# Second norm beside the output projection, early FFN loads, and a last down pass by column halves

## The chip, the cores and the metric

The kernel is one program that runs on all 8 cores of one Trainium2 chip at the same time. Each core computes half of one of the four samples; the cores do not exchange data. The metric is the device time of the slowest core, in microseconds (us). Such a program has two states. In the fast one all cores run alike. In the slow one the cores of a die, or of both, show a lower granted clock in the records and the time is longer.

I write PE for TensorE (matmul), ACT for ScalarE, DVE for VectorE, SP for SyncE (which here only issues DMAs) and POOL for GpSimd (which here issues the weight DMAs).

## The reference, cut to what matters

Two layers of a transformer block over 4 samples of 4096 latent tokens and 256 context tokens, width 2048, 12 query heads and 4 key/value heads of 128, FFN width 5632, everything modulated by a conditioning vector.

```python
xn = modulate(rms_norm(h, norm1_g), shift1, scale1)
y  = mixer(xn)                       # layer 0: dense attention + short conv; layer 1: windowed attention + pooling
h  = h + gate1 * (y @ w_out)         # output projection
hn = modulate(rms_norm(h, norm2_g), shift2, scale2)      # the "second norm"
h  = h + gate2 * ((silu(hn @ w_gate) * (hn @ w_up)) @ w_down)
...
return rms_norm(h, final_norm_g)     # after both layers
```

## The kernel before

Everything is kept transposed: 16 chunks of 128 channels on the partitions, tokens in the free dimension. Query blocks have 512 tokens (the last one of layer 0 has 384). One program-order list per engine is built in Python. A "main" generator (attention, FFN, projections) is woven with a "side" queue of generators, at a rate of side steps per main step.

```python
def weave(self, main, rate):
    credit = 0.0
    for _ in main:
        credit += rate
        while credit >= 1.0:
            credit -= 1.0
            if not self.step(): ...
```

The side generator of a block holds the output projection, then the norm of the same block. `Xb` is the residual stream of the block (16 chunks, one buffer), `hnst` two staging buffers of 4 chunks.

```python
def wout_gen(l, b, nblk, F, extra=None):
    for t in range(4):                      # 4 weight tiles w_out
        for c in range(4):                  # 4 output chunks each, 16 matmuls per chunk in 4 steps
            ...                             # DVE: Xb[dch] = psum * gate + Xb[dch]
    for _ in sq_gen(...): yield             # 16 squares (ACT and DVE in turn), 16 ones-matmuls to sum them
    rstd(...)
    for c in range(KD + 1):                 # apply1 on DVE, apply2 on ACT, store hn by 4 chunks
        ...
        if extra is not None and c % 2 == 0: next(extra, None)    # modulation of layer 1
    if b + 1 < nblk: load_Xb(l, b + 1)
```

The FFN of a token block loads all of its input `hn` at its start, runs gate/up and down for each half of the hidden width, and keeps the residual stream in HBM: in the down pass it loads, updates and stores tile by tile. The final norm of the last token block is done after everything else:

```python
side.weave(ffn_gen(side, 1, 1), 0.6)
side.drain()
for _ in final_gen(1):     # load 4 chunks, scale, store, one buffer
    pass
```

Weights come through a ring of three tiles (`NRING = 3`) on the POOL queue; all other transfers are issued by SP, in program order. A store can be held back by some steps: `sc.late(...)`, 24 by default, or until somebody wants to write its source buffer.

## Time and profile before

Before the prediction three runs stood at 7791, 7796 and 7899 us (median 7796.28).

The page of the slowest core, core 5: busy time of each engine in all, then two rows of the view in 40 slices, tenths of PE's busy share and tenths of full clock.

```profile
span 7794.5 us, 101076 instructions; the slowest of 8 cores (7745.4 to 7794.5 us)
...
PE 6943.4 (89%) x35368; PEld 3385.7 (43%) x35368; DVE 2287.2 (29%) x4515; ACT 2295.9 (29%) x3510; POOL 217.0 (3%) x262
...
PE   3889989999976999998999988968789999899992
...
PEclk9989999999998999999999999988889999999996
```

PE is the limit, and it stands still for 851 us of the span. The holes are at the start, in slice 12 (first FFN start), around slices 25 to 30 (layer 1's attention) and at the end. The clock sags where the holes are.

What PE waited for over the whole run, same core (columns: us in total, number of waits, longest):

```profile
PE pair L513 <- ACT arena L1009: 165.4, 181, 6.2
PE pair L513 <- DMA arena<-hn: 87.8, 3, 32.0
...
PE pair L513 <- DMA arena<-w_mod: 61.9, 9, 12.7
PE pair L513 <- DMA arena<-ud: 55.5, 4, 29.4
```

L1009 is the softmax exponential. `hn` is the FFN's input: three long waits, one at each FFN start that was not overlapped. `ud` is the pooling input of layer 1.

Stretches of the same core: from, to and length; busy us (and instructions) of PE, PEld, DVE, ACT and POOL; then granted clock, DMA share and GB/s.

```profile
core 5: us, PE busy (x) PEld busy (x) DVE busy (x) ACT busy (x) POOL busy (x), PEclk, DMA share, GB/s
1268.00:1447.00 179.00, 174.45 (x799) 77.10 (x799) 87.86 (x199) 127.43 (x135) 2.62 (x3) 1.00 0.38 93
1447.00:1562.00 115.00, 100.83 (x493) 41.03 (x493) 70.32 (x161) 102.61 (x124) 4.37 (x5) 0.97 0.80 170
...
5412.00:5553.00 141.00, 108.02 (x515) 49.80 (x515) 70.88 (x156) 68.73 (x142) 3.50 (x4) 0.85 0.68 160
...
7645.00:7794.00 149.00, 0.74 (x2) 0.13 (x2) 31.05 (x64) 4.98 (x6) 0.00 (x0) 0.51 0.36 116
```

The first two rows are one attention block of layer 0. Beside the output projection PE is full; then, beside the norm, ACT is the busiest (103 of 115 us), and over the block all PE waits that are listed are for the softmax exponential on ACT. The third is one block of layer 1, with no engine full. The last is the tail: PE is done, and the chain of waits goes load, scale, store, around and around:

```profile
7776.12 3.56 DMA arena<-hT
7782.11 2.95 DMA outT<-arena
7785.13 3.73 DMA arena<-hT
```

### The profile page before, as it was taken

What the parts mean: (1) busy time and instruction counts of PE and PEld (TensorE: products, weight loads), DVE (VectorE), ACT (ScalarE), POOL (GpSimd) and SP (SyncE); (2) the same over time, 40 slices, a digit from 0 to 9 for tenths busy, and PEclk for the clock granted to TensorE, in tenths of its full rate; (3) what the DMA queues carried; (4) which work ended last, traced back from release to release, by engine and by line L of the source; (5) the groups of instructions that cost most, each with busy time, mean ns of one, the idle gap of its engine ahead of it and who ended that gap; (6) DMA issues with size and microseconds to landing.
All of it is one profiled execution on the core that took longest, in us unless ns stands there. A gap on an engine that the chain in (4) does not pass through costs nothing.

```text
span 7794.5 us, 101076 instructions; the slowest of 8 cores (7745.4 to 7794.5 us)
## 1 busy us (share of the span) xinstructions
PE 6943.4 (89%) x35368; PEld 3385.7 (43%) x35368; DVE 2287.2 (29%) x4515; ACT 2295.9 (29%) x3510; POOL 217.0 (3%) x262
## 2 busy tenths in 40 slices
PE   3889989999976999998999988968789999899992
PEld 1334433343333555554555554433334444344441
DVE  1656455555531111111121113544521101111111
ACT  1655167878841100001110004544521000100000
POOL 0000000000000000000000000000000000000000
PEclk9989999999998999999999999988889999999996
DMA  9546873646676345345565365556764645648463
GB/s 176 142 108 118 144 158 88 140 116 137 138 160 137 71 103 130 65 99 138 99 160 114 64 171 119 116 116 149 154 145 89 156 86 111 136 85 190 93 156 105
DMA packets 486943, 971.21 MB, mean 125 GB/s; under 512 B 46256, under 2 KB 169904, under 8 KB 479024
## 3 DMA queue, kind: packets, MB, share of 16 engines
q0 software_dynamic: 233632, 495.76, 38.3%
q1 hardware_dynamic: 252816, 468.98, 18.8%
q8 instruction: 294, 4.82, 0.2%
q14 instruction: 201, 1.65, 0.1%
HBM read 1277.57 MB, written 182.85 MB: 187 GB/s over the span
## 4 chain that ended last, share of the span: by engine, by line
PE 81%; DMA 8%; ACT 4%; DVE 3%; issue 2%; SPq 2%; DVEq 0%; ACTq 0%; POOL 0%; POOLq 0%
PE pair L513 81%; ACT arena L1009 2%; SPq L199 2%; DMA arena<-w_mod 2%; DMA arena<-hT 2%; DMA arena<-w_in 1%; DMA arena<-hn 1%; DVE arena L587 1%; ACT arena L594 1%; DMA outT<-arena 1%; DMA arena<-w_gu 0%; DMA arena<-ud 0%; DVE arena L1475 0%; DMA arena<-kT 0%; DVE arena L1160 0%
## 5 line engine op out<-in xcount | busy, mean ns | idle before, releaser
L513 PE MATMUL pair<-arena 128*128 128x512 bf16 (+6 forms) x35368 | 6943.4, 361 | 703.7 <-ACT arena L1009 165.4
L513 PEld LDWEIGHTS pair<-arena 128*128 128x128 bf16 (+1 forms) x35368 | 3385.7, 100 | 4260.7 <-issue 1158.2
L1009 ACT ACTIVATE arena<-pair 128x1024 bf16<-128x1024 f32 (+3 forms) x1212 | 1009.6, 865 | 362.3 <-PE pair L513 308.3
L1369 ACT ACTIVATE arena<-pair 128x512 f32<-128x512 f32 (+3 forms) x440 | 239.6, 545 | 2847.0 <-PE pair L513 2847.0
L1372 DVE TENSOR_TENSOR arena<-pair,arena 128x512 bf16<-128x512 f32 (+3 forms) x440 | 274.8, 625 | 2470.5 <-PE pair L513 2461.1
L1018 DVE TENSOR_TENSOR arena<-arena 128x512 bf16<-128x512 bf16 (+2 forms) x1024 | 419.1, 410 | 523.6 <-ACT arena L1009 513.0
L1414 DVE SCALAR_TENSOR_TENSOR arena<-pair,arena 128x512 f32<-128x512 f32 (+3 forms) x352 | 225.7, 642 | 1096.7 <-PE pair L513 1062.9
L594 ACT ACTIVATE arena<-arena 128x512 bf16<-128x512 f32 (+6 forms) x448 | 281.6, 629 | 355.4 <-DVE arena L587 329.8
L587 DVE SCALAR_TENSOR_TENSOR arena<-arena 128x512 f32<-128x512 f32 (+6 forms) x448 | 279.9, 634 | 144.1 <-DMA arena<-hT 54.8
L1425 ACT ACTIVATE arena<-arena 128x1024 bf16<-128x1024 f32 (+2 forms) x64 | 72.8, 1137 | 666.5 <-DVE arena L1414 666.5
L1030 DVE TENSOR_TENSOR arena<-arena 128x512 bf16<-128x512 bf16 (+1 forms) x480 | 198.3, 413 | 63.9 <-DVE arena L1018 21.3
L695 DVE TENSOR_TENSOR arena<-pair,arena 128x512 f32<-128x512 f32 (+2 forms) x180 | 112.4, 625 | 209.7 <-PE pair L513 209.3
L1160 DVE SCALAR_TENSOR_TENSOR arena<-pair,arena 128x512 f32<-128x512 f32 (+2 forms) x160 | 109.5, 684 | 200.6 <-PE pair L513 197.4
L668 ACT ACTIVATE arena<-pair 128x512 bf16<-128x512 f32 (+2 forms) x180 | 97.4, 541 | 193.4 <-PE pair L513 193.4
L199 POOL DMA_DIRECT2D arena<-w_gu x88 | 77.0, 875 | 2413.1 <-PE pair L513 2331.3
L682 DVE SCALAR_TENSOR_TENSOR arena<-pair,arena 128x512 f32<-128x512 f32 (+2 forms) x180 | 122.8, 682 | 34.8 <-ACT arena L677 34.1
L697 DVE TENSOR_TENSOR arena<-arena 128x512 bf16<-128x512 f32 (+2 forms) x180 | 112.9, 627 | 52.8 <-DVE arena L695 31.4
L693 DVE TENSOR_TENSOR arena<-arena 128x512 f32<-128x512 f32 (+2 forms) x180 | 111.6, 620 | 53.0 <-ACT arena L687 52.6
L568 DVE TENSOR_TENSOR arena<-arena 128x512 bf16<-128x512 f32 (+2 forms) x144 | 92.9, 664 | 83.3 <-PE pair L513 56.5
L674 ACT ACTIVATE arena<-pair,arena 128x512 f32<-128x512 f32 (+2 forms) x180 | 113.5, 631 | 0.2 <-PE pair L513 0.2
L565 ACT ACTIVATE arena<-arena 128x512 bf16<-128x512 f32 (+2 forms) x144 | 84.3, 604 | 90.6 <-PE pair L513 62.3
L677 ACT ACTIVATE arena<-arena 128x512 f32<-128x512 f32 (+2 forms) x180 | 104.2, 579 | 16.8 <-ACT arena L674 0.4
(44 smaller groups left out, 852.8 us busy)
## 6 DMA issues: line engine op xcount, KB each, us to landing
arena<-w_gu POOLq DMA_DIRECT2D x88, 2048.0 KB, 15.2
arena<-w_mod POOLq DMA_DIRECT2D x48, 2048.0 KB, 19.7
arena<-w_down POOLq DMA_DIRECT2D x64, 1408.0 KB, 13.9
arena<-w_out POOLq DMA_DIRECT2D x36, 2048.0 KB, 19.8
arena<-hT SPq DMA_DIRECT2D x96, 512.0 KB, 6.3
arena<-w_in POOLq DMA_DIRECT2D x17, 2048.0 KB, 20.7
hT<-arena SPq DMA_DIRECT2D x32, 1024.0 KB, 9.6
hT<-arena SPq DMA_DIRECT2D x64, 512.0 KB, 5.7
```

The costliest lines, as they stand in the source:

```text
L199: e.dma_start(out=it[1], in_=it[2]).then_inc(it[3], 16)
L513: return e.matmul(out, lhsT=lhsT, rhs=rhs, start=start, stop=stop)
L587: sc.op("dve", lambda e, lo=lo, hi=hi, j=j: e.scalar_tensor_tensor(out=ta[:, lo:hi], in0=src[:, lo:hi], scalar=mcol(l, j, ps_, c), in1=rs[ ...
L594: sc.op("act", lambda e, lo=lo, hi=hi, j=j: e.activation(out=dst[:, lo:hi], in_=ta[:, lo:hi], func=AF.Identity, bias=mcol(l, j, pb_, c), s ...
L674: sc.op("act", lambda e: e.activation(out=tr[:, 0:n], in_=banks[SBK][:, 0:n], func=AF.Ln, bias=dcol(DC_CH), scale=1.0), reads=[s_bank[SBK] ...
L682: sc.op("dve", lambda e: e.scalar_tensor_tensor(out=tk[:, 0:n], in0=banks[pb][:, 0:n], scalar=dcol(gcol), in1=tr[:, 0:n], op0=ALU.mult, op ...
L1009: sc.op("act", lambda e: e.activation(out=dst, in_=src, func=AF.Exp, scale=float(ATT_SCALE)), reads=[s_bank[sb(gi, k)] for k in range(nb)] ...
L1018: sc.op("dve", lambda e, a=a % 4, w0=w0, w1=w1, m=m: e.tensor_tensor(out=ps1[a][:, 0:m], in0=P(w0[0], w0[1], m), in1=P(w1[0], w1[1], m), o ...
L1030: sc.op("dve", lambda e, b2=b2, a=arg[0] % 4, c=arg[1] % 4, m=m: e.tensor_tensor(out=ps2[b2][:, 0:m], in0=ps1[a][:, 0:m], in1=ps1[c][:, 0: ...
L1369: sc.op("act", lambda e, i=i, r=r, n=n: e.activation(out=sil[r][:, 0:n], in_=banks[2 * i][:, 0:n], func=AF.Silu), reads=[s_bank[2 * i]], w ...
L1372: sc.op("dve", lambda e, i=i, r=r, n=n, a=a, b=b, fi=fi: e.tensor_tensor(out=aT[fi][:, a:b], in0=banks[2 * i + 1][:, 0:n], in1=sil[r][:, 0 ...
L1414: sc.op("dve", lambda e, a=a, x0=x0, x1=x1, j=j, bk=bk, h=h, d=d: e.scalar_tensor_tensor(out=h[:, x0:x1], in0=banks[bk][:, x0 - a:x1 - a], ...
```

## The change

The intent: fill PE's holes. Six parts, which the diff mixes.

1. The squares of the second norm are made beside the output projection, chunk by chunk, and summed on DVE; one f32 matmul replaces 16. The scaling of block b runs beside the projection of block b+1. Side steps carry weights, and the attention says how much room it has.
2. `hn` is loaded in eighths, six or all eight of them before the FFN that needs them.
3. Layer 1: the attention's first loads come 14 items earlier, buffers are swapped, the pooling input is fetched a block ahead.
4. The start: weights before constants, norm steps between modulation steps, K before V in the first block.
5. The last down pass runs over one column half after the other with the stream in SBUF, so the first half is scaled and stored beside the second.
6. The norm and final-norm streams beside the FFN use two buffers of two chunks in place of one of four.

```diff
+    def norm2_gen(l, b, nblk):
+        for c in range(KD + 1):
+            ...                                   # apply1 (DVE), apply2 (ACT) into hnst, hn_store every 4 chunks
+            if c % 4 == 3 and b + 1 < nblk:
+                load_Xb(l, b + 1, c // 4)         # the next block's stream into the chunks just read
+            yield 0.7
-    def wout_gen(l, b, nblk, F, extra=None):
+    def wout_gen(l, b, nblk, F, extra=None, hook=None):
+        prev = norm2_gen(l, b - 1, nblk) if b > 0 else iter(())
+        for k in range(10):                       # the "lead"
+            if extra is not None:
+                if next(extra, 0) != 0:
+                    yield 1.0
+            c = next(prev, 0)
+            if c:
+                yield c
...
+                    if kq == 0:
+                        c_ = next(prev, 0)
+                    if kq == 1 and dch > 0:
+                        square(dch - 1)
+                    if kq == 2 and dch > 1:
+                        add(dch - 2)
...
-        for _ in sq_gen(n, lambda c: (Xb[:, c, 0:n], s_Xb[c]), TBs["sqn"], TBs["s_sqn"], F[0], 3):
-            yield
+        sc.op("pe", lambda e: mm(e, banks[bk][:, 0:n], one32[:, :], acc[:, 0:n], True, True), ...)
...
-        side.weave(ffn_gen(side, 0, 0, 24), 5.0)
+        side.weave(ffn_gen(side, 0, 0, 16, [lambda g=g: load_hn(0, 1, (g,)) for g in range(8)]), 5.0)
...
+        for si, (a, b) in enumerate(spl):         # last down pass: column halves
+            for t in range(8):
+                u = ws.take(W[l]["wd"][8 + t])    # w_down read again for the second half
+                ...
+                    if si == 1 and d > 0:
+                        scale(d - 1)              # first half: scale and store
...
-        side.add(final_gen(0))
-        side.weave(ffn_gen(side, 1, 1), 0.6)
+        side.add(final_gen())
+        side.weave(ffn_gen(side, 1, 1), 0.8)
         side.drain()
-        for _ in final_gen(1):
-            pass
```

## The prediction

> **What bounds it now.** Busy table: TensorE (PE) 6943 of 7794 us; VectorE (DVE), ScalarE (ACT) 29% each. In dense stretches a 512-column matmul starts every 0.215 us, and little matmul work is removed; to be won are PE's 850 us idle and its slow clock. Table of stretches and PE's waits:
> - head, 0-215 us: 135 idle (w_mod 60, constants 15, xn 15, w_in 14);
> - K/V projection, 215-540: 54 idle, clock 0.91;
> - layer-0 attention, 1270-2110: 53 idle. A block takes 294 us: 179 beside the output projection (PE 97% busy), then 115 in which second norm and softmax fill ACT (103 busy);
> - last block and FFN start, 2110-2520: 113 idle, 32 on hn loads;
> - FFN seams: 3605 (30, hn), 4500 (19, behind a queued load), 6695 (26, hn);
> - layer-1 projection, 4700-5110: 38;
> - its attention, 5110-5700: 172 idle, clock 0.76 to 0.85; three blocks of 142 us with PE work for about 93 (208 matmuls of 384 columns, 256 of 512);
> - end: PE stops at 7645, then 149 us of serial load, scale, store (chain of waits).
>
> The Trainium skill, "TensorE: Matmul & The Clock Gate", Part 1, says that idleness halves the clock and activity restores it; here dense FFN stretches show 1.00, layer-1 attention 0.83. Fewer gaps should pay twice.
>
> **The change, gains in us (estimates).**
> 1. Squares beside the output projection, scaling a block later, side steps weighted and spread. Per block 16 ones-matmuls (3.4 us PE) become one f32 matmul; DVE gains 15 adds of 0.65 us. The ACT-bound tail goes: PE about 261, ACT about 245 per layer-0 block, so 294 becomes 274: **60** for three. Layer 1 (pool input prefetched too) 142 to 109: **100**.
> 2. hn loads ahead, in eighths: last block and FFN start **75**, 3605 **30**, 6695 **25**, 5760 **10**; the blocking load at 4500 **18**.
> 3. Layer-1 attention's first loads 14 items earlier, off live buffers: **45**. Projection order (one weight tile less at once): **20**.
> 4. Head: weights before constants, norm between mods, K before V in block 0: **20**. Even K/V norm: **25**.
> 5. Last down pass by column halves: first half scaled and stored beside the second; about 25 us of scales and stores remain of 149. w_down is read twice: by the DMA table at 7480-7640 (8.65 MB weights = 31% of 160 us, 16.25 MB others = 29%), 23 MB and 17 MB need about 180 us DMA beside 152 PE; with three tiles prefetched, 10 us stall. Net **115**.
>
> Sum 543. Some gaps will move rather than vanish (ACT within 7% of PE in layer-0 attention; a drained norm at the layer-1 projection's seam): a tenth off.
>
> **Prediction: 7300 us, 80% range 7215 to 7400. Faster by over 2%: 0.96; within 2%: 0.03; slower: 0.01.**
>
> **What would show each step.** Layer-0 blocks near 274 us, layer-1 near 109, clock there above 0.92; waits on hn and ud nearly gone; PE dense across FFN seams; K/V blocks under 38 us (41 now); span end within 30 us of PE's last matmul, and in the last down pass short waits on w_down, DMA share over 0.9; DVE busy up by about 80 us; PE idle 350 to 450.
>
> **What would make it wrong.** The in-order DMA queue: an early hn load waiting for its buffer blocks later loads (waits on Xb, q, hb). Column halves DMA-bound (stall 40 us). Layer-0 attention staying bound by ACT's latency at 285 to 290, as scores lead by one pair only. Layer-1 attention bound by its exp-add-matmul chain rather than volume. Other way: clock recovery gives 50 us more.

## The result, and the profile after

The changed kernel runs in 7414.01 us (median of 4 runs, 7411.12 to 7527.89), the one before, with one more run on the same chip, in 7793.72. The ratio is 0.9527, with a 95% interval of 0.9499 to 0.9555. Ratios are the mean time of one kernel's fast runs over that of the other's of the same rounds, so not quite the ratio of these medians. The change is faster by 4.7%, and the forecast of 7300 was 114 us too low; 7414 lies 14 us outside the stated range.

The slowest core of the changed kernel is core 0:

```profile
span 7409.4 us, 101365 instructions; the slowest of 8 cores (7368.1 to 7409.4 us)
...
PE 6862.0 (93%) x35242; PEld 3354.3 (45%) x35242; DVE 2351.0 (32%) x4619; ACT 2278.3 (31%) x3526; POOL 227.3 (3%) x278
...
PE   3889999999977999999999999888789999999998
...
PEclk7999999999998999999999999999899999999999
```

The tail is filled and the clock has mostly come back, but PE is still idle for 547 us, where 350 to 450 was expected. The new list of PE's waits says with whom (lines have new numbers: L1034 is now the softmax exponential, L1252 the evacuation of the output projection, L604 the norm's second step on ACT, L597 its first on DVE):

```profile
PE pair L523 <- DMA arena<-w_mod: 115.6, 11, 39.2
PE pair L523 <- ACT arena L1034: 95.3, 136, 7.1
PE pair L523 <- ACT arena L604: 49.0, 9, 28.7
PE pair L523 <- DVE arena L1252: 40.1, 19, 20.8
...
PE pair L523 <- DMA arena<-hn: 11.4, 1, 11.4
```

The wait on `ud` is not in the list any more; `hn` fell from 88 to 11. But L1252, 31 us before, is at 40, with one wait of 21. `w_mod` has risen from 62 to 116, by 33 us at the start and 16 in block 4 of layer 0; the account of the prediction below comes back to the start. And L604 has one wait of 29 us, in the layer-1 projection, which the kernel before did not have.

The stretches that answer to those of before: one block of layer 0 whole, two blocks of layer 1, the second half of the last down pass, the tail.

```profile
core 0: us, PE busy (x) PEld busy (x) DVE busy (x) ACT busy (x) POOL busy (x), PEclk, DMA share, GB/s
1512.00:1789.00 277.00, 269.25 (x1290) 114.65 (x1279) 166.56 (x375) 228.83 (x259) 6.98 (x8) 1.00 0.58 134
5070.00:5181.00 111.00, 98.57 (x502) 47.08 (x502) 70.35 (x155) 55.88 (x126) 3.49 (x4) 0.95 0.68 149
5181.00:5309.00 128.00, 102.46 (x502) 47.68 (x502) 80.36 (x171) 67.14 (x143) 3.50 (x4) 0.88 0.73 175
...
7304.00:7389.00 85.00, 81.55 (x377) 36.06 (x375) 22.67 (x32) 13.31 (x20) 4.44 (x6) 1.00 0.90 189
7389.00:7409.00 20.00, 0.24 (x1) 0.00 (x0) 11.35 (x17) 1.32 (x2) 4.37 (x8) 0.53 0.63 236
```

The block of layer 0 is now PE-bound from end to end. The two blocks of layer 1 have the same 502 matmuls, yet one takes 111 us and the other 128. The end of the chain of waits is now ten scales on DVE and one store:

```profile
7395.64 5.97 DVE arena L1559 x9
7402.02 2.97 DMA outT<-arena
```

**Where the time went, by stretch.** I cut both traces at events that both kernels have, such as the first softmax exponential of a block, the first Silu of an FFN half, PE's last matmul. A "seam" is the change from one token block of the FFN to the next, or to the next stage. The table gives the median over the 8 cores; most rows agree between cores within a few us.

| stretch | before | after | gain | predicted |
|---|---|---|---|---|
| start to first Q projection | 539.6 | 520.6 | 19 | 45 |
| Q projection and layer-0 block 0 | 701.8 | 699.2 | 3 | 0 |
| layer-0 blocks 1 to 3 | 881.5 | 837.6 | 44 | 60 |
| layer-0 block 4 | 182.0 | 152.7 | 29 | 75 with the next row |
| its last exponential to half 1 of the first FFN | 694.8 | 695.3 | 0 | |
| half 1 of the first FFN, and the seam | 617.1 | 587.6 | 30 | 30 |
| layer 0, second token block, half 0 | 514.8 | 539.1 | -24 | 0 |
| the same, half 1, and the seam | 548.6 | 523.6 | 25 | 18 |
| layer-1 projection | 452.8 | 425.3 | 28 | 20 |
| layer-1 block 0 | 98.9 | 66.7 | 32 | 45 |
| layer-1 blocks 1 to 3 | 425.4 | 361.3 | 64 | 100 |
| last exponential to half 1 of layer 1's first FFN | 542.5 | 549.3 | -7 | 10 |
| half 1, and the seam | 497.4 | 469.6 | 28 | 25 |
| layer 1, second token block, up to the last Silu | 753.0 | 767.9 | -15 | 0 |
| last down pass | 166.1 | 170.6 | -5 | -10 |
| PE's last matmul to the end | 147.3 | 22.1 | 125 | 125 |

The gains sum to 376 us; the spans themselves fell by 373 (medians 7760.8 and 7387.9). So the question is not whether the change works but where some 165 of the 543 us of listed gains went.

Two pairs of rows must be read together, because the event between them moved against PE's work:

- Block 4 and the row after it. After the change 50 of the 256 matmuls of block 3's projection (11 us at 0.215 us each, an estimate) run after block 4's last exponential; before, none did. So 11 of the 29 us were only moved into the next row, whose length hides that PE's idle time there fell from 66 to 55 us. Together the two rows gave 29.
- The two halves of layer 0's second token block. The first Silu of half 1 comes 13 us after PE's first matmul of that half, in place of 3. Cut at that matmul, half 0 grew by 12 us (519 to 531) and not by 24. Together the two rows are unchanged, 1064.7 and 1064.2 us.

Three places stand out: the start of layer 0's FFN, where the table shows no gain; two rows that got longer; and layer 1's blocks 1 to 3, of which only the first came near the forecast.

### The profile page after: what moved, and what is told of

Read it like the earlier page. It is cut to its first block, busy times and chain, and to the rows that moved or that the text cites. A ratio compares the mean times of both kernels' runs of the same rounds, so it can differ in the third digit from the quotient of the medians.

```text
span 7409.4 us, 101365 instructions; the slowest of 8 cores (7368.1 to 7409.4 us)
## 1 busy us (share of the span) xinstructions
PE 6862.0 (93%) x35242; PEld 3354.3 (45%) x35242; DVE 2351.0 (32%) x4619; ACT 2278.3 (31%) x3526; POOL 227.3 (3%) x278
## 4 chain that ended last, share of the span: by engine, by line
PE 82%; DMA 9%; ACT 3%; DVE 3%; issue 2%; SPq 1%; another core or an unknown queue 0%; DVEq 0%; ACTq 0%; POOLq 0%
PE pair L523 82%; DMA arena<-w_mod 2%; DMA arena<-w_out 1%; DMA outT<-arena 1%; ACT arena L604 1%; ACT arena L1034 1%; DMA xn<-arena 1%; SPq L199 1%; DMA arena<-kT 1%; DVE arena L597 1%; DMA hn<-arena 0%; DMA arena<-hT 0%; DMA arena<-w_down 0%; DMA arena<-w_in 0%
## 5 line engine op out<-in xcount | busy, mean ns | idle before, releaser
L523 PE MATMUL pair<-arena 128*128 128x512 bf16 (+5 forms) x35242 | 6862.0, 360 | 527.3 <-DMA arena<-w_mod 115.6
L1034 ACT ACTIVATE arena<-pair 128x1024 bf16<-128x1024 f32 (+3 forms) x1212 | 1011.7, 866 | 259.8 <-PE pair L523 187.0
L1519 DVE SCALAR_TENSOR_TENSOR arena<-pair,arena 128x428 f32<-128x428 f32 (+3 forms) x320 | 201.4, 630 | 846.0 <-PE pair L523 841.6
L604 ACT ACTIVATE arena<-arena 128x512 bf16<-128x512 f32 (+6 forms) x448 | 280.5, 627 | 317.9 <-DMA xn<-arena 161.2
L597 DVE SCALAR_TENSOR_TENSOR arena<-arena 128x512 f32<-128x512 f32 (+6 forms) x448 | 279.5, 634 | 238.0 <-ACT arena L604 170.5
L1530 ACT ACTIVATE arena<-arena 128x1280 bf16<-128x1280 f32 (+2 forms) x48 | 55.8, 1163 | 498.0 <-DVE arena L1519 498.0
L1252 DVE SCALAR_TENSOR_TENSOR arena<-pair,arena 128x512 f32<-128x512 f32 (+2 forms) x160 | 109.5, 684 | 125.1 <-PE pair L523 121.5
L707 DVE TENSOR_TENSOR arena<-arena 128x512 bf16<-128x512 f32 (+2 forms) x180 | 112.8, 627 | 45.7 <-DVE arena L705 30.6
L703 DVE TENSOR_TENSOR arena<-arena 128x512 f32<-128x512 f32 (+2 forms) x180 | 111.5, 619 | 37.2 <-ACT arena L697 31.9
L697 ACT ACTIVATE arena<-arena 128x512 bf16<-128x512 f32 (+2 forms) x180 | 101.5, 564 | 13.8 <-DVE arena L692 13.7
L199 POOL DMA_DIRECT2D arena<-w_down x72 | 53.4, 742 | 1574.2 <-PE pair L523 1519.4
```

The lines of the kernel that those rows point to most:

```text
L199: e.dma_start(out=it[1], in_=it[2]).then_inc(it[3], 16)
L523: return e.matmul(out, lhsT=lhsT, rhs=rhs, start=start, stop=stop)
L597: sc.op("dve", lambda e, lo=lo, hi=hi, j=j: e.scalar_tensor_tensor(out=ta[:, lo:hi], in0=src[:, lo:hi], scalar=mcol(l, j, ps_, c), in1=rs[ ...
L604: sc.op("act", lambda e, lo=lo, hi=hi, j=j: e.activation(out=dst[:, lo:hi], in_=ta[:, lo:hi], func=AF.Identity, bias=mcol(l, j, pb_, c), s ...
L1034: sc.op("act", lambda e: e.activation(out=dst, in_=src, func=AF.Exp, scale=float(ATT_SCALE)), reads=[s_bank[sb(gi, k)] for k in range(nb)] ...
L1519: sc.op("dve", lambda e, a=a, x0=x0, x1=x1, j=j, bk=bk, h=h, d=d: e.scalar_tensor_tensor(out=h[:, x0:x1], in0=banks[bk][:, x0 - a:x1 - a], ...
```

## The experiments

All runs computed the right result. Unless said otherwise numbers are medians over all 8 cores of the profiled run, cut as in the table. The four runs of the first call ran on a chip whose second die was disturbed, so cores 0 to 3 are used; blocks 2 and 3 of layer 0 were some 4 to 7 us slower there in all four, so they are compared within the call.

The first theory: **a convoy on SP's in-order list**, that is, transfers held up behind one that waits. (`hT` is the residual stream in HBM, `xn` the input of layer 1, `outT` the result.) In the stretch that grew from 515 to 539 us, ACT and DVE wait like this (the down pass of the changed kernel, 3840 to 4060 us):

```profile
ACT arena L604 <- DMA xn<-arena: 161.2, 7, 33.2
DVE arena L597 <- ACT arena L604: 83.5, 7, 17.1
...
PE pair L523 <- DVE arena L1519: 11.0, 4, 5.3
```

and SP's own list, same stretch, has

```profile
SPq L195 <- DVE arena L1519: 153.1, 16, 18.4
```

Read as a ring: the store of `xn` stands behind stores of the stream, which wait on SP for the down pass's evacuation (DVE L1519); that evacuation stands on DVE behind a norm step (L597) that waits for ACT; ACT waits for the `xn` store. The rivals were DMA bandwidth, and that the side's work costs its time wherever it runs.

### r1_hold: no side steps in the first down passes

```diff
                         if si < len(spl) - 1:
-                            yield
+                            yield (0.0 if half == 0 and tb == 1 else None)
...
-                    yield
+                    yield (0.0 if half == 0 and tb == 1 else None)
...
-        side.weave(ffn_gen(side, 1, 1), 0.8)
+        side.weave(ffn_gen(side, 1, 1), 1.15)
```

> The changed kernel, but no side step runs beside the first down pass of layer 0's second token block and of layer 1's second one (its steps run beside the gate/up passes instead). In the changed kernel these two stretches (gate/up of one half plus its down pass, from first Silu of half 0 to first Silu of half 1) take 539 and 464 us (means of 8 cores) against 515 and 456 before. Theory A, a convoy on the in-order queue that carries both the stream's tiles (hT) and the side's tiles (xn, outT): 515 and 456 again, the gate/up stretches that take over the steps unchanged, total 30 us less (about 7383). Rival B, the side's own work or bytes cost the time wherever they run: the first stretches fall, the second halves (523 and 297) grow by the same, total unchanged within 8 us.

Measured, cores 0 to 3: layer 0's stretch 514.3, the next one 529.0 (523.6 before the edit); layer 1's 456.0 and 297.0 (from 464.2 and 306.7). The two passes are as short as in the kernel before, and 5 us of the 43 came back. These 5 are the shifted event again: with the side held off, the first Silu of half 1 is back at 3 us after PE's first matmul, and the two rows of layer 0 together take 1044.5 us (1064.2 before the edit). The net gain is 20 us in layer 0 and 18 in layer 1. The rival that the work costs its time anywhere is refuted. What remained open was whether it was the queue or the bytes.

### r1_actq: only the xn stores on another queue

```diff
-                sc.late("sp", xn_d[2 * g:2 * g + 2 ...
+                sc.late("act", xn_d[2 * g:2 * g + 2 ...
```

> The changed kernel with only the side's xn stores issued from the ACT queue instead of the SP queue; same bytes, same order of compute. Theory A (xn stores stand in the queue behind the stream's stores, ACT waits for their buffer, VectorE behind ACT, and the down pass's evacuation behind VectorE): the stretch of 539 us in layer 0's second token block falls to under 522, ACT's wait on xn (161 us in that down pass) falls to under 40; layer 1's stretch (464) does not change, since nothing of it was touched. Rival (DMA bandwidth, 0.84 share there): 539 stays within 4.

Measured: 514.1 us, the whole 25 us, with the same bytes and the same compute; the two rows together take 1044.3 us, so 20 us net, as in r1_hold. ACT's wait on `xn` fell from 161 to 42 us, just above the 40 that was expected:

```profile
ACT arena L604 <- DMA xn<-arena: 42.2, 4, 13.7
```

Layer 1's stretch, untouched, did not fall (471.9; 464 to 471 in all other runs that did not hold the side). On core 0, from 3840 to 4060 us, SP issued an `xn` store a median of 7.9 us after the last norm step on ACT before it, and ACT issued it 0.1 us after; from issue to landing it took 10.7 us and then 7.1. So the cause in layer 0 is mainly the place in SP's list: most of what a store lost, it lost before it was issued, not in the transfer. For layer 1's second token block the same kind of cause is visible but not separated: SP there waited 105 us for stores of `outT` in the first down pass, and holding the side off the pass cured it.

The second theory was about layer 1's blocks and the FFN start. The changed kernel at the start of layer 1's second full block:

```profile
5203.05 1.53 ACT L604 ACTIVATE arena<-arena 128x512 bf16<-128x512 f32 x2 [0.25 <-DVE arena L597]
...
5213.80 0.72 ACT L604 ACTIVATE arena<-arena 128x512 bf16<-128x512 f32 x1 [8.84 <-DMA hn<-arena]
5214.43 0.47 ACT L1034 ACTIVATE arena<-pair 128x384 bf16<-128x384 f32 x1
...
5215.05 1.12 PE L523 MATMUL pair<-arena 128*128 128x384 bf16 x3 [7.12 <-ACT arena L1034]
```

(A line of the timeline: start, length, engine, instruction, and in brackets the idle time before it and what ended it.) ACT stands 8.8 us before a norm step, for a store of `hn`; the next softmax exponential stands behind it, and PE behind that. The Trainium skill, "PSUM — Partial Sum Buffer", "Engine vs sequencer instructions", calls the queues of ScalarE and VectorE "strict FIFO"; these lines agree: an exponential whose scores are ready (PE had stood still since 5207.93 us) waits at least 6.5 us for a step that has nothing to do with it. My first guess was the queue again.

### r2_hnq: the hn stores on the ACT queue (a miss)

```diff
-        sc.late("sp", hn_d[d - 3:d + 1 ...
+        sc.late("act", hn_d[d - 3:d + 1 ...
```

> The changed kernel with only the stores of the second norm's result (hn) issued from the ACT queue instead of the SP queue. Theory A (the store stands in the SP queue behind loads of x that wait for VectorE; ACT waits for its staging buffer; then VectorE and PE): the wait of ACT on the hn store at the start of the FFN (15 us, PE idle 21 us behind it) goes, last block to first FFN (211 us from the block's first exp to the first Silu) becomes about 192; layer 1's second and third full blocks (128 and 122 us) lose the 9 and 6 us of that wait and become about 118 and 115, total about 30 to 35 us less. Rival B (these blocks are long because of the amount of norm work on ACT and VectorE, whatever the queue): blocks unchanged within 3 us, only the 15 us at the FFN start move.

Measured, cores 0 to 3: blocks 126.3 and 123.0, unchanged. The store wait at the FFN start stayed (13.2 us on core 0). Worse, the first FFN halves grew: from the first Silu to half 1, 647 us against 636 in layer 0 and 537 against 518 in layer 1, where PE now waited 13 us for a Silu, which stands on ACT behind the store's wait. The theory fell: the queue was not what the store was waiting for.

### r3_mod: modulation tiles spread over the projection (a miss)

```diff
-            if extra is not None:
-                if next(extra, 0) != 0:
-                    yield 1.0
             c = next(prev, 0)
...
+                if extra is not None and dch % 2 == 1:
+                    if next(extra, 0) != 0:
+                        yield 1.0
```

> The changed kernel with the modulation tiles of layer 1 spread over the output projection (one step every second output chunk) instead of in its first ten steps. Theory A (four w_mod tiles and the first w_out tile are asked of a ring of three within about 30 us, which the DMA cannot give): in the last layer-0 block the PE waits on w_mod (16 us) and w_out (7 us) fall to under 6 together and the block (157 us) takes about 140; the three full blocks lose a few us (284, 277, 279 to about 275). Rival B (the last block is short of DMA in total, share 0.93 there): the waits only move to other tiles and the block stays within 5 us.

Measured, cores 0 to 3: block 4 took 152.1 us (153.1 and 154.7 in two other runs on this chip), blocks 1 to 3 279.5, 281.4 and 283.2 (283.5, 282.0, 285.2 with the side held off). The waits on w_mod and w_out in block 4, 24 us in the changed kernel, are gone. Others took their place, on core 0 from 2065 to 2220 us:

```profile
PE pair L523 <- ACT arena L1034: 17.2, 10, 8.8
PE pair L523 <- DVE arena L1114: 15.2, 9, 2.6
```

L1114 is the last step of an attention unit. So the longest named wait of that block was not what sets its length. What does was not tested.

### r5_late: the early hn loads undone

```diff
-        if tb == 0:
-            load_hn(l, tb, (6, 7))
+        load_hn(l, tb, range(8))
...                                     # and no load_hn anywhere else
```

> The changed kernel with the early loads of the FFN input hn undone: all eight pieces are loaded at the start of each FFN block, none before. If the early loads are what closed the seams: first Silu to first Silu of the next block grows again by what the change took away, 588 to about 617 in layer 0's first block and 470 to about 497 in layer 1's (both seams lie at the end of those stretches); from the last exp of layer 0 to the first Silu 59 to about 90, and of layer 1 30 (to the FFN's first Silu) plus 20; total 90 to 110 us more. Rival (the narrower pieces and the drained side explain it, not the early start): the two later seams grow by less than 10 each.

Measured: the two later seams grew as expected, 587.6 to 614.7 and 469.6 to 497.5. At layer 0's first FFN the early loads are worth 4.4 us before the first Silu and 2.6 after it, not 30; in layer 1's 3.7 and 0.2. The total rose by 89 us (other chip; expected 90 to 110), some 66 of it in these four places. So the early loads are the cause of the seams' gains and do next to nothing at the two FFN starts that follow attention.

Why is seen in the waits at layer 0's FFN start. Before the change (2329 to 2560 us):

```profile
PE pair L513 <- DMA arena<-hn: 32.0, 1, 32.0
```

After it (2225 to 2490 us):

```profile
PE pair L523 <- DVE arena L1252: 36.4, 14, 20.8
```

The evacuation of the last projection's first chunk needs the stream in `Xb`, and `Xb` is freed only by the scaling of the block before, which now runs here, with no attention beside it.

### r7_lead: a shorter lead

Theory C, formed after r2_hnq: the lead of ten norm steps is a burst. Its ninth step fills a third group of four chunks, and there are two staging buffers. The store of the first group is held back until exactly that step asks for the buffer, and then ACT waits a whole round trip.

```diff
-        for k in range(10):
+        for k in range(10 if extra is not None else 6):
```

> The changed kernel with the lead of the second norm's steps before the output projection cut from ten to six where no modulation steps go with them (layer 1, and layer 0's last block). Theory C, formed after the run with the stores on the ACT queue failed: the lead is a burst; its ninth step needs the staging buffer that its fourth step filled, of two buffers, so ACT waits a whole store (9, 6 and 15 us) and the burst itself holds the softmax up. With six steps no third buffer is needed within the burst: the eight groups at the start of a layer-1 block that took 25.6 and 23.2 us take about 14, the second and third full blocks (127, 122) fall to 115 or less, near the first one (112), which has no second norm; the wait of 15 us at layer 0's FFN start goes and last exp to first Silu falls from 59 to about 42. Total about 30 to 35 us less. Rival B (the amount of norm work, not its bunching, costs 10 to 15 us): the blocks stay within 4 us of 127 and 122.

Measured: 115.1 and 111.5 us for the second and third full block, from 127.3 and 122.2. Norm work is the same; only its bunching changed. The volume rival is refuted. The run as a whole took 7399.48 us in its one fast execution, 12 us less than the 7411.12 of the changed kernel's profile and not the 30 to 35 expected; on this chip layer 1's second token block and the last down pass were 5 to 12 us longer also in r5_late and r8_now, so totals of different chips are not compared further. At the FFN start the gain was 10 us, in two parts (59.0 to 54.3 and 635.2 to 630.0), less than the 17 expected before the first Silu alone.

### r8_now: the store not held back

```diff
-                f"hnst{h}", [s_hnst[h]], [sd(f"hn{l}_{b}")])
+                f"hnst{h}", [s_hnst[h]], [sd(f"hn{l}_{b}")], 0)
```

> The changed kernel with the hn stores issued as soon as their four chunks are computed instead of being held back up to 24 steps; the lead of ten stays. If the held-back issue is most of the wait: ACT's waits on the hn store (15 us at the FFN start, 9 and 6 in layer 1) fall by half or more and the blocks (127, 122) by 4 to 6 us, the stretch last exp to first Silu (59) by about 8; total 15 us less. If it is the store's own round trip or the burst: blocks within 2 us.

Measured: 121.6 and 118.3 us, 6 and 4 less, and 57.5 at the FFN start (59.0). In the blocks holding back the store was 36 to 47% of what r7_lead won; the rest needs the burst itself shortened.

### r11_head: projection steps before the FFN cut

With the short lead PE still stands at the FFN start (core 7 of r7_lead, 2258 to 2285 us):

```profile
PE pair L523 <- DVE arena L1252: 13.6, 1, 13.6
...
DVE arena L1252 <- DMA arena<-x: 10.2, 1, 10.2
```

This is a new serial chain that the later scaling made: scale four chunks, reload the buffer, evacuate.

```diff
-        side.weave(ffn_gen(side, 0, 0, 16, ...), 5.0)
+        side.weave(ffn_gen(side, 0, 0, 7, ...), 5.0)          # with r7_lead's edit
```

> The short lead as before, and the steps of layer 0's last projection that run ahead of the FFN cut from 16 to 7. With the short lead the PE still stands 13.6 us at the FFN start, behind VectorE, which waits 10 us for the x piece that the one-block-late scaling frees only then. Theory: it is a serial chain (scale four chunks, reload the buffer, evacuate) with nothing beside it because the FFN has not begun; with FFN matmuls issued sooner the PE has work in it: from the last block's last exp to the second half's first Silu (54 plus 630 in the run with the short lead) 8 to 14 us less, the waits on VectorE's evacuation there under 10. Rival (in PE's in-order program the blocked projection matmul just comes later and blocks as long; or the FFN's own hn pieces are not in yet): within 4 us.

This chip's first die was disturbed; cores 4 to 7 are used. The wait of 13.6 is gone (the longest on L1252 is now 1.3 us), but last exponential to half 1 is 706 us (42.1 and 664.4) against 684 with the short lead. Three others came, on core 4 from 2220 to 2560 us:

```profile
PE pair L523 <- DMA arena<-w_gu: 12.4, 1, 12.4
PE pair L523 <- ACT arena L1474: 9.9, 1, 9.9
PE pair L523 <- DMA arena<-hn: 9.1, 1, 9.1
```

The theory was right on the chain and wrong on its worth. The run cannot tell whether the three waits stood behind the chain all along or were made by the new order, in which tiles of the projection and of the FFN take turns in the ring of three.

### r9_tail: the last part undone

```diff
-        final = l == 1 and tb == 1
+        final = False
...
         side.drain()
+        for _ in final_gen(1):
+            pass
```

> The changed kernel with its last part undone: the last down pass goes tile by tile over all columns again, stores its stream, and the final norm is done after it, by load, scale and store (in the changed kernel's pieces of two chunks, double buffered). The last down pass, from the last Silu to PE's last matmul, falls from 171 to 166 us (w_down read once), and from there to the end grows from 22 us to between 100 and 147 (147 before, single buffered). Total 75 to 120 us more. If the tail were not serial in load and store, it would grow by less than 60.

Measured: the last down pass 166.0 (170.6), the tail 126.4 us (22.1). Net of the 5 us that the second reading of w_down costs, the column halves are worth 100 us against a double-buffered serial tail, and 121 against the old single-buffered one (125 less 5, from the table).

### r12_xlate: the second block's x after the first weight tile

```diff
-                    if c % 2 == 1 and c < 15:
-                        load_x(1, c // 2 + 1)
-            load_x(2, 0)
...
+                if i == 0:
+                    aft = [] if sc.plan else [s_ring[ws.slot[ws.used]]]
+                    for g in range(1, 8):
+                        load_x(1, g, aft)
+                    load_x(2, 0, aft)
```

> The changed kernel with the eight x pieces for the second K/V block held back until the first K/V weight tile (w_in) has landed. In the changed kernel the first K projection's square comes 166 to 168 us after the start (159 before), although its w_in tile is asked for in the same place of the weight stream; by then 9.7 MB of x and tables have landed beside the weights, 7.7 MB before, with all DMA engines busy throughout. Theory (the head is bound by bytes, and the x pieces of the second block, 4 MB, now go ahead of the weight tile): the first square comes at 153 to 160 us. What it gives back: the second block's norm waits for its x, so the K/V stage (354 us) grows by about as much, and the start of the Q projection (520 us) stays within 5 us. Rival (the order of the modulation steps, norm steps between them on the in-order engines, delays the stream): first square within 3 us of 167.

Measured: the first square at 161.8 us (166.0), the K/V stage 359.7 (354.1), and the Q projection starts at 520.6 us, as in the changed kernel. It moved in the direction of the byte theory but by 4 us, short of the 6 to 13 expected, so part of the later start has another cause that is open. That it is all given back was as expected.

### c_after and r10_both: the two corrections together

r10_both is the changed kernel with the edits of r1_hold and r7_lead; c_after is the changed kernel as control on the same chip.

> The changed kernel unaltered, as control for the runs of this call on the same chip: stretches within 3 us of its first profile, fast runs near 7414, ratio to the kernel before near 0.953.

> The two corrections together: side steps held off the first down passes (as in the run that held them) and the norm's lead cut to six where no modulation goes with it. If the causes are independent, the gains add: 539 to 514, 464 to 456 and 307 to 297 for the held side, less 5 given back in the next stretch; 127 to 115 and 122 to 112 for the lead, and about 9 at layer 0's FFN start; fast runs near 7350 against about 7414, ratio to the kernel before near 0.944 against 0.953. If they overlap, less than 45 us of it.

That chip was slow in most executions; each of the two has one fast run, 7414.40 (c_after) and 7343.39 (r10_both), and the kernel before has fast runs from 7758 to 7829. With one fast run each there is no interval. Their ratio is 0.990; 7343.39 over the mean of the four fast runs before (7758.36, 7766.68, 7768.48, 7829.23) is 0.944. The control repeats the first profile's stretches within 4 us, but for layer 1's second token block, 8 us longer as a whole. The stretches, on 8 cores each, add up as expected: 538.4 to 514.0, 467.9 to 456.1, 307.6 to 297.0, with 5 given back by the shifted event; 126.4 to 114.6 and 122.0 to 109.4; 59.3 to 52.5 and 638.4 to 629.9. The median core fell from 7400.6 to 7323.9. In these runs this version beats both kernels, and the undisturbed dies of the slow executions agree: their cores took 7299 to 7344 us, those of the control 7366 to 7394. The blocks of layer 1 with it:

```profile
core 2: us, PE busy (x) PEld busy (x) DVE busy (x) ACT busy (x) POOL busy (x), PEclk, DMA share, GB/s
5043.00:5155.00 112.00, 99.05 (x502) 46.89 (x502) 70.25 (x155) 56.08 (x127) 3.50 (x4) 0.95 0.70 147
5155.00:5270.00 115.00, 99.09 (x502) 47.09 (x502) 80.26 (x172) 66.68 (x145) 3.51 (x4) 0.96 0.81 194
```

## Why the prediction was wrong, point by point

**Right: direction, and the parts where one wait stood alone.** (3605, 4500, 5760 and 6695 are times in the trace before.) The tail (121 net, predicted 115), the seams at 3605 and 6695 (30 and 28; 30 and 25) and the blocked load at 4500 (20 net of the convoy, 1064.7 to 1044.5 in r1_hold; 18) came as stated. Layer 1's projection and block 0, where a wait of 29 us on `ud` went, gave 60 together (65). For the tail and the seams r9_tail and r5_late show by undoing them that the named parts are the cause; the blocked load, the projection order and part 3 of the change were undone by no run. In the last down pass the DMA share was 0.99 and then 0.90 (forecast: over 0.9), but PE waited for w_down only 0.8 us in all, where 10 was forecast.

**Right: the mechanism in the blocks.** The ACT-bound end of layer 0's blocks is gone; the blocks take 277 to 283 us for the 274 forecast, 44 us in place of 60. DVE gained 64 us, predicted 80. In layer 1 the first block with a projection takes 112, predicted 109.

**Wrong: the step "Sum 543. Some gaps will move rather than vanish ... a tenth off".** The tenth, 50 us, should have been about 165. Its parts, with what the runs showed in their place:

- *"last block and FFN start 75".* Together they gave 29. I counted the full wait on `hn` as gain. It vanished, and behind it stood the chain of scaling, reload and evacuation that part 1 of the change itself had moved to this place, where no attention hides it. PE's idle time in the start row fell only from 66 to 55 us. r5_late: the early loads are worth 7 us here. r7_lead: a shorter burst is worth 10. r11_head: with the chain's wait removed by a new order, three other waits of 31 us appear, and the stretch is 22 us longer.
- *Two passes of the FFN that I had not listed at all* lost 24 and 15 us in the table, 20 and 15 net of the shifted event. I had named the in-order queue as a risk, but for the `hn` loads; it struck in the streams beside the down passes. r1_actq shows the cause in layer 0 (20 us net for moving one kind of store off SP's list), r1_hold removes both.
- *"Layer 1 142 to 109: 100".* It gave 64, since only the first of three blocks had no second norm beside it. r7_lead: the loss was the burst of ten steps with two staging buffers, not the amount of work; with six steps the blocks are 112 to 115.
- *"Head 20, even K/V norm 25".* 19 in place of 45. The part that failed is the head. Cut at the first square of a K projection, the K/V stage gave 26 us (380 to 354), as forecast, and the head gave -7. In both kernels the DMA engines are full up to there (28.8 MB by 155 us before, 30.2 MB by 166 after), so the new order only renamed PE's waits: on w_mod 60 us became 94, on steps of ACT 40 became 4. r12_xlate gave back 4 of the 7. In the K/V stage blocks take 39 us (354 over 9), where 38 was my limit.
- *"5760: 10"* became -7. PE waits there 11 us for the last two `hn` pieces, whose buffers are free only after attention, and 5 for w_gu. Read from the trace, not tested.
- *"a drained norm at the layer-1 projection's seam"*, one of the gaps that I named as likely to move, is there: on core 0 one PE wait of 28.7 us on L604, near 4800 us, and 28 us on cores 1, 3 and 5 too. It alone is more than half of the tenth that I took off. It is the longest PE wait after the start and stands in r1_actq and r10_both as well; no run removed it.

**The clock** did follow the gaps. The Trainium skill, "TensorE: Matmul & The Clock Gate", Part 1, says that idle windows halve PE's clock and busy ones restore it. The trace agrees: on core 0 of the changed kernel the granted clock is at every moment either full or half, and a layer-1 block had 0.82 to 0.85 before, and 0.95, 0.88 and 0.87 after, where the first is the one without the burst; with the burst gone all are at 0.95 or 0.96. I had forecast above 0.92 for all.

**Open.** Whether the queue, or something else beside the down pass, was layer 1's 15 us. The wait of 28.7 us in the layer-1 projection, which a run could attack first. What sets the length of layer 0's block 4 (r3_mod removed its longest waits in vain). What remains at layer 0's FFN start, and layer 1's 7 us; about 3 of the 7 us of the later start; and the layer-0 blocks' distance from their matmul time. That time is 258 us by an estimate from the trace (1180 matmuls of 512 columns at the median start-to-start of 0.215 us, plus small ones), against 277.

## What to carry to other kernels

A list of waits is not a list of gains: a wait's whole length is won only where nothing stands behind it, so for each gap ask what the engine would have waited for next, and trust only the gaps with a full buffer behind them. Work moved to a later place takes its buffers with it: check the last block, where the cover it relies on has ended. A burst of side steps that reaches round its ring of staging buffers makes an in-order engine wait a whole store, and everything queued on that engine with it; keep a lead shorter than the ring. And where a trace is cut into stretches at an event of one engine, check the cut at another: an event that is itself delayed makes one stretch longer and the next one shorter, with no work moved.

## What the Trainium skill lacked or had wrong

- "DMA: Bandwidth & Descriptors", "Issuing engines are not separate DMA queues", says that issuing from several engines "will only save the time on the sequencer it takes to initiate the DMA, which is usually small relative to the DMA itself". In r1_actq moving one kind of store from SP to ACT saved 20 us of 1064, since the store no longer stood in one program with waits of other transfers. The page lacks that an issuing engine's waits block its later transfers.
- The same page's "Rules for kernel authors" advises to issue a DMA early and wait late. It held at two seams (27 and 28 us in r5_late) and hardly at two other places (7 and 4 us), and it does not say that holding a store back has a price: 6 and 4 us per block in r8_now.
- "TensorE: Matmul & The Clock Gate", "Seeing it yourself", says to budget 1.95 GHz, 13/16 of full clock, for sustained dense matmul on all cores on the default power profile (which profile these chips had is not on record). Here the 8 cores together ran at a mean granted clock of 0.971 to 0.975 in the fast run of 7411 us; a die near 0.835 was seen only in slow runs (8386 us in one of r7_lead).
